# Streaming encoder step: earlier weight splits, an earlier kv norm, keys before queries, and inputs and outputs in pieces of their own

## The chip, the cores and the metric

The kernel runs on one core of one Trainium2 chip. The metric is the device time of one execution in microseconds (us). TensorE (PE) multiplies, VectorE (DVE), ScalarE (ACT) and GpSimd (POOL) do the rest, SyncE (SP) issues the DMAs. Each engine runs its own instructions in the order in which the program emits them, and waits on semaphores for the others.

## What is computed

One layer, on 512 new positions (a prompt) and on 64 new positions that have a past of 128 (a sample): RMSNorm, one input projection, two attention groups side by side, an output projection with a residual, RMSNorm, a gated feed-forward part with a causal convolution, a residual and a last RMSNorm. The second attention group, the latent one, is where most of the change lies:

```python
c_q  = rmsnorm(proj[..., OFF_CQ:OFF_CKV], g_qa)
c_kv = rmsnorm(proj[..., OFF_CKV:OFF_KR], g_kva)
k_r  = rope(proj[..., OFF_KR:IN_COLS], pos)
q_m  = (c_q @ w_qb).reshape(B, T, MLA_HEADS, MLA_NOPE + MLA_ROPE)
q_nope, q_rope = q_m[..., :MLA_NOPE], rope(q_m[..., MLA_NOPE:], pos)
ckv_all = jnp.concatenate([p_ckv, c_kv], axis=1)     # the sample's cache ahead
kv = (ckv_all @ w_kvb).reshape(B, Tk, MLA_HEADS, MLA_NOPE + MLA_V)
k_nope, v_m = kv[..., :MLA_NOPE], kv[..., MLA_NOPE:]
```

## The kernel before

Tokens lie along the free axis: 576 of them (512 and 64), worked on in two groups of 256 and 320 columns (GRP). Every product is made in three passes to keep float32's accuracy: an operand is split into a high part (a cast on ACT) and a low part (the difference, on DVE), and `mm3` (line 136) adds hi x hi, hi x lo and lo x hi in PSUM. So every weight tile of 128x1024 costs two casts on ACT and two subtractions on DVE of 128x512 each (`Weights.split_hi`, line 123, `split_lo`, line 127). A weight has a raw buffer (tag wraw, three of them) and a high and a low one (whi, wlo, four each).

The stages:
1. Lines 195 to 310: the input x (eight tiles of 128 features) and the first key weights are loaded, scaled and split, and the first key pair is multiplied tile by tile (`k_step`, line 263). The squares for the first norm are made beside it.
2. Lines 905 to 1140: 28 attention blocks in slots. A slot combines the block before (softmax scaling), begins a block (scores on PE, maximum on DVE, exponential on ACT), transposes the block before and multiplies values for the one before that. Between these, a planner (`Filler`, line 938) puts the projections that later blocks need, as generators that yield after every few products: V0, K1, Q1, V1, CQ (query latent), CKV (kv latent), KR (rotary key), QU (rotary queries from the latent), U0 to U3 (one head each: queries without rotation and keys, `head_up`, line 716), VM (latent values, `v_up`, line 742), W0 to W3 (output projection).
3. From line 1144 on: the second half of the output projection, the feed-forward part and, in `down(..., last)` from line 1385 on, the last products, the last norm and the stores.

The order on every engine is that of emission as far as stage 2 and again in the last part. In `Filler.step` (line 985) each call counts one step: first the side chains that are due go on by one piece (`beside`, line 972; a chain says with `yield n` in how many steps it wants to go on), then perhaps one half of a weight split is emitted, then the next product. Which weights are split ahead is set by `self.ahead` (those of the next item) and by `SPLIT_EVERY`, every how many steps; what isn't ready when its item begins is split there in one go. `POOL_SPLITS` sends low parts to POOL during CQ and CKV. A weight's load is issued when an earlier weight is ready.

The latent norm is such a side chain (`Latent.normalize`, line 600): squares on ACT, `NORM_STEPS[0]` steps later the column sums on PE (`sum_cols`, line 162: ten matmuls with one column each for one tile of 576), then the root (`rsqrt_cols`, line 171: a memset on POOL, a scaling on DVE, a power on POOL), then a spread over the partitions by PE (`spread`, line 185, tile rbc) and the scaling on DVE, and the split of the result. For kv, `kv_finish` (line 644) first splits the cache part. The rotary key (`rotary_key`, line 651, `shared_key`, line 667) makes two products on DVE and two sums on POOL for each column group (tile kro). Accumulators of tag acc rotate through three PSUM buffers: products, column sums and spreads all use them.

Of the kernel before, what the change touches and what calls it, by code (L numbers as in the profile page):

```python
# [47 lines left out]
Y_GAINS = {4: (0, 2), 5: (2, 3), 6: (3, 4), 7: (4, 5)}  # L48
# [17 lines left out]
def stream_step(ctx: ExitStack, tc: tile.TileContext, i, o):  # L66
# [141 lines left out]
    pieces = [slice(0, 256), slice(256, 512), slice(512, 1024)]  # L208
    w_k = [Weights(i["w_in"][n], 1024, f"wk{n}", pieces) for n in range(2)]
    w_q = [Weights(i["w_in"][2 + n], 1024, f"wq{n}", 2) for n in range(2)]  # L210

    def load_x(c0, c1):
        nc.sync.dma_start(out=xall[:, c0:c1], in_=i["xT"][:, c0:c1])

    def load_tile(k):
        load_x(KD + k * T, KD + (k + 1) * T)
# [12 lines left out]
    w_k[1].load(2)  # L229
    for k in (5, 6, 7):  # L230
        load_tile(k)
# [56 lines left out]
    wsteps = {1: [(0, 1), (1, 1)], 3: [(0, 2)], 4: [(1, 2)]}  # L288
    for k in range(1, KD):
        x_hi(k, full)  # L290
        for n, part in wsteps.get(k, ()):
            w_k[n].split_hi(part)
        if k >= SQUARES_BEHIND:
            square(k - SQUARES_BEHIND)
        x_lo(k, full)
        for n, part in wsteps.get(k, ()):
            w_k[n].split_lo(part)
# [288 lines left out]
    class Latent:  # L586
# [13 lines left out]
        def normalize(self):  # L600
            yield 1
            sqs = []
            for c in self.raws:
                sq = tmp("lsq")
                nc.scalar.activation(out=sq[:, :T], in_=c[:, :T], func=AF.Square)
                sqs.append(sq)
            yield NORM_STEPS[0]
            pc = sum_cols(sqs, T, "acc")
            yield NORM_STEPS[1]
            rc = rsqrt_cols(pc, T, self.n)  # L610
            yield NORM_STEPS[2]
            for c0, cn in GRP:
                pb = spread(rc, c0, cn)
                for m, c in enumerate(self.raws):
                    stt(c[:, c0:c0 + cn], c[:, c0:c0 + cn], vec[:, self.gcol + m:self.gcol + m + 1],
                        pb[:, :cn], ALU.mult, ALU.mult)
                yield NORM_STEPS[3]
# [14 lines left out]
    def q_finish():  # L632
        yield from lat_q.normalize()
# [82 lines left out]
    def head_up(h):  # L716
        if h == 0:
            lw["qns"] = att.tile([P, HEADS, DEC], F32, tag="xs", name="qns")
        ql = lw["qnl", h] = tmp("qnl", (P, SEQ), dt=F32R)
        kl = lw["knl", h] = tmp("knl", (P, SEQ), tag="cs" if h < 2 else "rtab", bufs=2, dt=F32R)  # L720
        for c0, cn in GRP:
# [20 lines left out]
    def v_up(wkv):
        vm = lw["vm"] = att.tile([P, 6, 512], F32, tag="vd", name="vm")
        for t in range(6):
# [6 lines left out]
            nc.scalar.copy(out=vm[:m, t, :], in_=acc[:m])  # L751
# [163 lines left out]
    def w_in(idx, n=2):  # L915
        return [(i["w_in"][idx + m], 1024, f"wi{idx + m}") for m in range(n)]
# [21 lines left out]
    class Filler:  # L938
# [46 lines left out]
        def step(self):  # L985
# [4 lines left out]
            if self.gen is None:  # L990
# [11 lines left out]
                self.finish(*{"QU": ["q"], "U0": ["kv"]}.get(self.name, []))  # L1002
# [391 lines left out]
    def down(s, act, last):  # L1394
# [56 lines left out]
        for f in range(KD):  # L1451
            e0, e1 = Y_GAINS.get(f, (0, 0))

            def before():
                for e in range(e0, e1):
                    scale(1, rn, e, e + 1)
# [6 lines left out]
            if e1 and e1 % 2 == 0:  # L1463
                store(1, e1 - 2, e1)
        scale(1, rn, 5, 6)
        store(1, 4, 6)
        nrm.finish()
        rn0 = nrm.spread()
        scale(1, rn, 6, 8)
        store(1, 6, 8)  # L1470
# [72 lines left out]
def _layout(a):  # L1543
# [3 lines left out]
    d["xT"] = np.ascontiguousarray(np.concatenate(  # L1547
        [a["g_attn"][0].reshape(KD, P).T, x.T.reshape(KD, P, T).transpose(1, 0, 2).reshape(P, KD * T)], 1))
# [9 lines left out]
    d["w_in"] = np.stack([_ktiles(t) for t in tiles])  # L1558
# [18 lines left out]
    for s, n in enumerate(SEGS):  # L1577
# [22 lines left out]
         "conv": (P, NJ, 4), "y": (P, KD, T)}  # L1600
# [25 lines left out]
```

## Time and profile before

| | |
|---|---|
| median of 3 runs | 678.63 us (678.11 to 681.22) |
| profiled execution | 678.01 us |
| its span, first to last instruction | 676.2 us |
| mean granted TensorE clock | 0.992 |
| PE busy | 657.4 us |
| DVE, ACT, POOL busy | 507.3, 314.1, 120.4 us |
| DMA | 63.63 MB, mean 94 GB/s |

How to read it: the span is what the trace covers, and the sum is made against the profiled execution. A PE busy for 97% is bound by its products or by their clock; where it is idle, the list of waits names the engine and line that it waited for. A line can be that of a helper (L84 is every two-operand operation, L87 every one with a scalar, L139 to L141 every three-pass product), so groups go by tile. The granted clock is a share of 2.4 GHz: 1.00 or 0.50 (1.2 GHz), and values between are means over a stretch.

### The profile page before, as it was taken

How to read it: one execution, taken by the hardware profiler on the slowest of the kernel's cores; microseconds unless marked ns; L12 is line 12 of the kernel's file. 1: busy time of each engine (PE TensorE's matmuls, PEld its weight loads, DVE VectorE, ACT ScalarE, POOL GpSimd, SP SyncE). 2: the span in 40 equal slices, each digit the busy share in tenths (PEclk: the TensorE clock that was granted, in tenths of full speed). 3: DMA queues.
4: the chain of work that ended last, by engine and by line, in shares of the span. 5: the costliest groups of instructions: out<-in, count | busy, mean ns of one | idle time of the engine just before them, and what ended most of it. 6: DMA issues, size and time to landing. Idle time of an engine off the chain costs nothing.

```text
span 676.2 us, 12353 instructions
## 1 busy us (share of the span) xinstructions
PE 657.4 (97%) x4830; PEld 632.7 (94%) x4830; DVE 507.3 (75%) x1022; ACT 314.1 (46%) x622; POOL 120.4 (18%) x170
## 2 busy tenths in 40 slices
PE   9999999997899999999999999999999999999995
PEld 8998898996799899999999999999999999999994
DVE  6768866588677757899999849984894788697634
ACT  7324345344634346375565236532640552464263
POOL 0130213034200016232230101210120010011042
PEclk9999999999999999999999999999999999999997
DMA  8564413012514103003133303430431134124103
GB/s 297 176 178 136 133 44 117 12 32 90 200 35 143 45 32 126 1 18 108 63 126 125 126 1 126 125 103 24 126 127 60 48 110 125 36 76 143 32 1 141
DMA packets 26826, 63.63 MB, mean 94 GB/s; under 512 B 3216, under 2 KB 8272, under 8 KB 26768
## 3 DMA queue, kind: packets, MB, share of 16 engines
q1 hardware_dynamic: 26768, 62.84, 28.8%
q8 instruction: 38, 0.62, 0.4%
q14 instruction: 20, 0.16, 0.1%
HBM read 55.27 MB, written 5.21 MB: 89 GB/s over the span
## 4 chain that ended last, share of the span: by engine, by line
PE 85%; DVE 8%; ACT 2%; issue 1%; POOL 1%; DMA 1%; SPq 0%; DVEq 0%; POOLq 0%; ACTq 0%
PE yacc L139 9%; PE yacc L140 9%; PE yacc L141 9%; PE ua L1251 6%; PE ua L1249 6%; PE ua L1250 6%; PE ub L1251 3%; PE ub L1250 3%; PE ub L1249 3%; PE uc L1251 2%; PE uc L1250 2%; PE uc L1249 2%; PE S L490 1%; PE uplain L139 1%; PE tp L467 1%
## 5 line engine op out<-in xcount | busy, mean ns | idle before, releaser
L84 DVE TENSOR_TENSOR x<-x,yacc 128x288 f32<-128x288 f32 (+2 forms) x128 | 56.4, 451 | 49.4 <-PE yacc L141 49.1
L139 PE MATMUL yacc<-act,wd 128*128 128x288 f32 x288 | 85.2, 296 | 0.0
L141 PE MATMUL yacc<-act,wd 128*128 128x288 f32 x288 | 85.1, 296 | 0.0
L140 PE MATMUL yacc<-act,wd 128*128 128x288 f32 x288 | 85.1, 295 | 0.0
L141 PEld LDWEIGHTS yacc<-act,wd 128*128 128x128 f32 x288 | 54.3, 188 | 0.1
L140 PEld LDWEIGHTS yacc<-act,wd 128*128 128x128 f32 x288 | 54.3, 189 | 0.0
L139 PEld LDWEIGHTS yacc<-act,wd 128*128 128x128 f32 x288 | 54.3, 189 | 0.0
L1277 POOL COPY cst<-G 128x2 f32<-128x2 f32 x22 | 19.6, 889 | 164.9 <-DVE G L84 149.0
L458 ACT ACTIVATE p<-S,nmax 128x128 f32<-128x128 f32 (+4 forms) x36 | 18.5, 515 | 42.2 <-DVE nmax L456 41.8
L1338 ACT COPY u<-ua 128x288 f32<-128x288 f32 x20 | 8.0, 399 | 63.9 <-PE ua L1251 63.9
L87 DVE SCALAR_TENSOR_TENSOR conv<-G,vec,conv 128x578 f32<-128x578 f32 x44 | 35.9, 816 | 2.0 <-ACT conv L1282 2.0
L1264 POOL COPY G<-zero 128x2 f32<-128x2 f32 x22 | 14.0, 636 | 130.4 <-DVE conv L87 121.8
L84 POOL TENSOR_TENSOR n<-n,nsq 128x288 f32<-128x288 f32 x13 | 12.3, 950 | 75.3 <-ACT nsq L866 75.1
L1282 ACT ACTIVATE conv<-G,vec 128x578 f32<-128x578 f32 x22 | 19.2, 872 | 8.8 <-DVE G L84 8.7
L458 ACT ACTIVATE p<-Sm,nmax 128x128 f32<-128x128 f32 (+4 forms) x18 | 9.3, 515 | 29.1 <-DVE nmax L456 29.1
L84 POOL TENSOR_TENSOR st<-pr 128x256 f32<-128x256 f32 (+1 forms) x16 | 13.4, 858 | 50.1 <-issue 16.9
L90 ACT CAST act<-conv 128x576 fp32r<-128x576 f32 x22 | 14.9, 675 | 12.7 <-DVE conv L84 12.6
L1286 ACT ACTIVATE silu<-conv 128x578 f32<-128x578 f32 x22 | 15.2, 689 | 11.0 <-DVE conv L87 11.0
L470 DVE COPY pT<-tp 128x128 f32<-128x128 f32 (+3 forms) x36 | 16.7, 463 | 4.3 <-PE tp L467 3.8
L866 ACT ACTIVATE nsq<-x 128x288 f32<-128x288 f32 (+2 forms) x28 | 12.3, 444 | 16.1 <-DVE x L84 16.0
L456 DVE TENSOR_REDUCE nmax<-S 128x1 f32<-128x128 f32 (+4 forms) x36 | 17.0, 476 | 1.1
L467 PE MATMUL tp<-ident,p 128*128 128x128 f32 x84 | 15.5, 277 | 2.3 <-DVE Sm L454 1.0
(1595 smaller groups left out, 2554.8 us busy)
## 6 DMA issues: line engine op xcount, KB each, us to landing
qkT<-st SPq DMA_DIRECT2D x32, 72.0 KB, 2.1
x<-in_xT SPq DMA_DIRECT2D x4, 576.0 KB, 6.4
xraw<-in_xT SPq DMA_DIRECT2D x7, 288.0 KB, 5.3
out_y<-x SPq DMA_DIRECT2D x4, 320.0 KB, 2.3
out_kd<-st SPq DMA_DIRECT2D x4, 288.0 KB, 2.4
out_vp<-vd SPq DMA_DIRECT2D x2, 512.0 KB, 4.7
out_y<-x SPq DMA_DIRECT2D x2, 384.0 KB, 2.7
wq0r<-in_w_in SPq DMA_DIRECT2D x2, 256.0 KB, 5.9
```

The lines of the kernel that those rows point to most:

```text
L84: (eng or nc.vector).tensor_tensor(out=out, in0=a, in1=b, op=op)
L87: nc.vector.scalar_tensor_tensor(out=out, in0=a, scalar=s, in1=b, op0=op0, op1=op1)
L139: nc.tensor.matmul(out, lhsT=wh, rhs=xh, start=first, stop=False)
L140: nc.tensor.matmul(out, lhsT=wh, rhs=xl, start=False, stop=False)
L141: nc.tensor.matmul(out, lhsT=wl, rhs=xh, start=False, stop=last)
L458: nc.scalar.activation(out=p[:, :nk], in_=Sv, func=AF.Exp, bias=nmax[:, 0:1], accum_out=sums)
L467: nc.tensor.transpose(out=pt_ps[:, n * P:n * P + P], in_=a[:, c:c + P], identity=ident)
L1249: nc.tensor.matmul(acc, lhsT=wh, rhs=xh, start=first and n == 0, stop=False, skip_group_check=True)
L1250: nc.tensor.matmul(acc, lhsT=wh, rhs=xl, start=False, stop=False, skip_group_check=True)
L1251: nc.tensor.matmul(acc, lhsT=wl, rhs=xh, start=False, stop=(n == len(ks) - 1), skip_group_check=True)
L1277: nc.gpsimd.tensor_copy(out=cst[:, j, 0:2], in_=G[:, 512:514])
L1282: nc.scalar.activation(out=c[:, :578], in_=G[:, 0:578], func=AF.Identity, scale=cw[0], bias=cb)
```

## The change

1. Weight splits: `POOL_SPLITS` goes, all low parts are on DVE. A table AHEAD names, for CQ to U0, which weights are split during an item, and `SPLIT_EVERY` has other counts.
2. The kv norm has its own, shorter counts, and the split of the cache part is a side chain of its own that begins with the kv products.
3. `head_up` makes the keys of the prompt first, then the queries, then the sample's keys.
4. `v_up` copies its results out of PSUM by ACT and DVE in turn.
5. The input x comes as three tensors, each read at a stretch. The first two key weights come together, two feature tiles at a time from tile 2 on, into buffers of the later softmax. The residual reads x in nine loads, not four.
6. The last scaling writes a tile of its own, in pieces that are contiguous, and each piece is an output tensor. The second group's scalings and stores are done in pairs while the first group's products run.

```diff
-NORM_STEPS = (3, 1, 4, 2)
+NORM_STEPS, KV_STEPS = (3, 1, 4, 2), (2, 1, 3, 1)
-SPLIT_EVERY = {"V1": 3, "U1": 2, "KR": 2, "CKV": 3, "QU": 3, "U0": 2}
-POOL_SPLITS = ("CQ", "CKV")
+SPLIT_EVERY = {"V1": 3, "U1": 2, "CQ": 2, "KR": 2, "QU": 2, "U0": 2}
+AHEAD = {"CQ": ("wi10", "wkr"), "CKV": ("wqr", "wqn"), "KR": ("wkv",), "QU": ("wo0",), "U0": ("wo0",)}
-Y_GAINS = {4: (0, 2), 5: (2, 3), 6: (3, 4), 7: (4, 5)}
+Y_GAINS = {4: (0, 2), 5: (2, 4), 6: (4, 6), 7: (6, 8)}
...
+    def k_load(k, kn=1):
+        nc.sync.dma_start(out=k_cols(k_raw, k, kn), in_=i["w_k1"][k] if kn == 1 else i["w_k2"][k // 2 - 1])
...
-    load_x(0, KD + GRP[1][0])
-    w_k[0].load(0)
-    w_k[1].load(0)
-    load_x(KD + GRP[1][0], KD + T)
+    nc.sync.dma_start(out=xall[:, :KD + GRP[1][0]], in_=i["x_a"])
+    k_load(0)
+    nc.sync.dma_start(out=xraw[:, 0, GRP[1][0]:], in_=i["x_b"])
+    k_load(1)
     load_tile(1)
-    w_k[0].load(1)
-    w_k[1].load(1)
+    k_load(2, 2)
     load_tile(2)
     load_tile(3)
-    w_k[0].load(2)
+    k_load(4, 2)
     load_tile(4)
-    w_k[1].load(2)
-    for k in (5, 6, 7):
-        load_tile(k)
+    load_tile(5)
+    k_load(6, 2)
+    load_tile(6)
+    load_tile(7)
...
-    wsteps = {1: [(0, 1), (1, 1)], 3: [(0, 2)], 4: [(1, 2)]}
+    k_parts = {1: 1, 2: 2, 4: 2, 6: 2}
     for k in range(1, KD):
+        if k in k_parts:
+            k_split_hi(k, k_parts[k])
         x_hi(k, full)
...
-        def normalize(self):
+        def normalize(self, wait):
...
     def kv_latent(ws):
         nc.sync.dma_start(out=kro[:DEC, T:TK], in_=i["c_kr"])
         cc = tmp("cc", (P, P), tag="rd", bufs=2)
         nc.sync.dma_start(out=cc, in_=i["c_ckv"])
+        filler.beside("cc", split_later(ckv[:, 0, T:TK], ckv[:, 1, T:TK], cc))
         yield from lat_kv.project(ws[0])
-        filler.beside("kv", kv_finish(cc))
+        filler.beside("kv", kv_finish())
-    def kv_finish(cc):
-        yield from split_later(ckv[:, 0, T:TK], ckv[:, 1, T:TK], cc)
-        yield from lat_kv.normalize()
+    def kv_finish():
+        yield from lat_kv.normalize(KV_STEPS)
...
+        keys(0, SEQ)
+        yield 3 * SEQ / 2400 + 0.1
         for c0, cn in GRP:
             acc = psum("acc", "qnacc")
...
+        keys(SEQ, PAST + DEC)
+        yield 3 * (PAST + DEC) / 2400 + 0.1
...
-            nc.scalar.copy(out=vm[:m, t, :], in_=acc[:m])
+            if t % 2:
+                nc.vector.tensor_copy(out=vm[:m, t, :], in_=acc[:m])
+            else:
+                nc.scalar.copy(out=vm[:m, t, :], in_=acc[:m])
...
-        for m in range(0, KD, 2):
-            nc.sync.dma_start(out=x1[:, m:m + 2],
-                              in_=i["xT"][:, KD + m * T:KD + (m + 2) * T].rearrange("p (k t) -> p k t", k=2))
+        nc.sync.dma_start(out=x1[:, 0, :GRP[1][0]], in_=i["x_a"][:, KD:])
+        nc.sync.dma_start(out=x1[:, 0, GRP[1][0]:], in_=i["x_b"])
+        for m in range(1, KD):
+            nc.sync.dma_start(out=x1[:, m], in_=i["x"][m - 1])
...
-            if half == w.split_lo and self.name in POOL_SPLITS:
-                half(part, nc.gpsimd)
-            else:
-                half(part)
+            half(part)
...
+                if self.name in AHEAD:
+                    self.ahead = [w for w in self.loaded if w.name in AHEAD[self.name]]
...
+        yo = sb.tile([P, KD * T], F32, tag="M", bufs=2, name="yo")
+        ys = [yo[:, KD * c0:KD * (c0 + cn)].rearrange("p (f t) -> p f t", f=KD) for c0, cn in FG]
...
-            y = x1[:, f:e, c0:c0 + cn]
-            tt(y, y, rn[:, :cn].unsqueeze(1).broadcast_to([P, e - f, cn]), ALU.mult)
+            tt(ys[grp][:, f:e], x1[:, f:e, c0:c0 + cn], rn[:, :cn].unsqueeze(1).broadcast_to([P, e - f, cn]), ALU.mult)
-            nc.sync.dma_start(out=o["y"][:, f:e, c0:c0 + cn], in_=x1[:, f:e, c0:c0 + cn])
+            nc.sync.dma_start(out=o[f"y{grp}_{f}"], in_=ys[grp][:, f:e])
```

## Rows read from the trace of the kernel before

**Rows 1.** The page, part 1: busy us, share of the span, instructions of each engine.

```profile
PE 657.4 (97%) x4830; PEld 632.7 (94%) x4830; DVE 507.3 (75%) x1022; ACT 314.1 (46%) x622; POOL 120.4 (18%) x170
```

**Rows 2.** Stretches: length, busy us of each engine (instructions), PE clock, DMA share, GB/s.

```profile
130.00:140.00 10.00, 10.00 (x72) 8.44 (x72) 5.34 (x16) 3.53 (x8) 2.76 (x4) 1.00 0.03 9
140.00:150.00 10.00, 10.00 (x83) 9.32 (x82) 9.66 (x22) 7.48 (x18) 2.74 (x3) 1.00 0.17 53
150.00:160.00 10.00, 8.13 (x60) 7.64 (x58) 8.70 (x19) 3.53 (x5) 6.27 (x7) 1.00 0.43 152
160.00:170.00 10.00, 8.07 (x45) 6.97 (x44) 7.33 (x19) 4.46 (x15) 3.63 (x4) 0.86 0.09 23
170.00:180.00 10.00, 8.89 (x57) 7.26 (x55) 6.71 (x19) 6.53 (x24) 2.55 (x3) 0.97 0.32 105
```

**Rows 3.** Waits of PE: engine, line, tile, releaser: us in total, times, longest.

```profile
PE qracc L139 <- DVE pr L87: 1.9, 1, 1.9
PE Sm L764 <- ACT knp L738: 1.2, 1, 1.2
...
PE vmacc L748 <- ACT vm L751: 0.6, 1, 0.6
...
PE Sm L765 <- DVE knl L84: 0.4, 1, 0.4
```

**Rows 4.** Stretches of 2 us, as rows 2.

```profile
168.00:170.00 2.00, 2.00 (x8) 1.75 (x8) 1.02 (x4) 0.72 (x4) 0.00 (x0) 0.50 0.43 113
```

**Rows 5.** Timeline of DVE, 146 to 154 us: start, us, instruction [idle before <- releaser].

```profile
146.38 0.68 DVE L84 TENSOR_TENSOR wqrl<-wqrr,wqrh 128x512 fp32r<-128x512 f32 x1
...
147.40 0.43 DVE L84 TENSOR_TENSOR pr<-kracc,sinr 64x256 f32<-64x256 f32 x1
147.86 1.96 DVE L84 TENSOR_TENSOR lat<-lc,lat 128x576 fp32r<-128x576 f32 x2
150.60 0.15 DVE L177 TENSOR_SCALAR ms<-ncol 64x1 f32<-64x1 f32 x1 [0.79 <-POOL ms L176]
...
152.45 1.95 DVE L84 TENSOR_TENSOR wqnl<-wqnr,wqnh 128x512 fp32r<-128x512 f32 x2
```

**Rows 6.** Timeline of PE, KR to the first latent scores.

```profile
145.06 0.36 PE L139 MATMUL kracc<-xh,wkrh 128*128 128x256 f32 x1
...
148.29 1.15 PE L167 MATMUL ncol<-ones,lsq 128*128 128x1 f32 x10
149.37 0.41 PE L139 MATMUL kracc<-xh,wkrh 128*128 128x320 f32 x1
...
151.23 0.28 PE L139 MATMUL qracc<-lat,wqrh 128*128 128x256 f32 x1
...
165.95 0.33 PE L765 MATMUL Sm<-knl,qn 128*128 128x128 f32 x1 [0.40 <-DVE knl L84]
```

**Rows 7.** Timeline of ACT, 145 to 147 us.

```profile
145.39 0.62 ACT L125 CAST wqrh<-wqrr 128x512 fp32r<-128x512 f32 x1
145.90 0.69 ACT L605 ACTIVATE lsq<-lc 128x576 f32<-128x576 f32 x1
```

**Rows 8.** Timeline of POOL, 147 to 153 us.

```profile
147.91 2.50 POOL L84 TENSOR_TENSOR kro<-pr 32x256 f32<-32x256 f32 x2 [7.18 <-DVE pr L84]
150.47 0.10 POOL L176 MEMSET ms<- 128x1 f32 x1
150.97 1.48 POOL L84 TENSOR_TENSOR rc<-ms,mhalf 128x5 f32<-128x5 f32 x1 [0.40 <-DVE ms L179]
```

**Rows 9.** Timeline of ACT at the third x tile.

```profile
8.39 0.78 ACT L252 ACTIVATE xh<-xraw 128x576 fp32r<-128x576 f32 x1 [1.03 <-DMA xraw<-in_xT]
```

**Rows 10.** Stretches of 1 us, as rows 2: head with small and larger pieces, tail.

```profile
5.00:6.00 1.00, 1.00 (x7) 1.00 (x6) 0.55 (x1) 0.20 (x2) 0.00 (x0) 1.00 1.02 281
12.00:13.00 1.00, 1.00 (x10) 1.00 (x9) 0.80 (x2) 1.00 (x3) 0.00 (x0) 1.00 1.03 402
672.00:673.00 1.00, 0.00 (x0) 0.00 (x0) 0.23 (x1) 0.00 (x0) 0.00 (x0) 0.50 1.00 336
```

More of the change, by code (lines that the diff above doesn't have):

```diff
@@ L207, in stream_step, with k_cols, k_split_hi, k_split_lo @@
     xraw = xall[:, KD:].rearrange("p (k t) -> p k t", k=KD)
[L208 to L213, printed above, removed]
-    def load_tile(k):
-        load_x(KD + k * T, KD + (k + 1) * T)
-    load_x(0, KD + GRP[1][0])
-    w_k[0].load(0)
-    w_k[1].load(0)
-    load_x(KD + GRP[1][0], KD + T)
+    k_raw = [att.tile([P, 512], F32, tag="P", bufs=4, name=f"wkr{m}") for m in range(4)]
+    k_hi = [sb.tile([P, 1024], F32R, tag="whi", bufs=4, name=f"wkh{m}") for m in range(2)]
+    k_lo = [sb.tile([P, 1024], F32R, tag="wlo", bufs=4, name=f"wkl{m}") for m in range(2)]
+    w_q = [Weights(i["w_in"][n], 1024, f"wq{n}", 2) for n in range(2)]
+    def k_cols(tiles, k, kn=1):
+        at = k * 256 % tiles[0].shape[1]
+        return tiles[k * 256 // tiles[0].shape[1]][:, at:at + kn * 256]
+    def k_load(k, kn=1):
+        nc.sync.dma_start(out=k_cols(k_raw, k, kn), in_=i["w_k1"][k] if kn == 1 else i["w_k2"][k // 2 - 1])
+    def k_split_hi(k, kn=1):
+        nc.scalar.copy(out=k_cols(k_hi, k, kn), in_=k_cols(k_raw, k, kn))
+    def k_split_lo(k, kn=1):
+        tt(k_cols(k_lo, k, kn), k_cols(k_raw, k, kn), k_cols(k_hi, k, kn).bitcast(F32), ALU.subtract)
+    def load_tile(k):
+        nc.sync.dma_start(out=xraw[:, k], in_=i["x"][k - 1])
+    nc.sync.dma_start(out=xall[:, :KD + GRP[1][0]], in_=i["x_a"])
+    k_load(0)
+    nc.sync.dma_start(out=xraw[:, 0, GRP[1][0]:], in_=i["x_b"])
+    k_load(1)
     load_tile(1)
-    w_k[0].load(1)
-    w_k[1].load(1)
+    k_load(2, 2)
     load_tile(2)
     load_tile(3)
-    w_k[0].load(2)
+    k_load(4, 2)
     load_tile(4)
-    w_k[1].load(2)
-    for k in (5, 6, 7):
-        load_tile(k)
+    load_tile(5)
+    k_load(6, 2)
+    load_tile(6)
+    load_tile(7)
     w_q[0].load(0)
@@ L295, in stream_step @@
         x_lo(k, full)
-        for n, part in wsteps.get(k, ()):
-            w_k[n].split_lo(part)
+        if k in k_parts:
+            k_split_lo(k, k_parts[k])
         if k > ADDS_BEHIND:
@@ L606, in normalize @@
                 sqs.append(sq)
-            yield NORM_STEPS[0]
+            yield wait[0]
             pc = sum_cols(sqs, T, "acc")
-            yield NORM_STEPS[1]
+            yield wait[1]
             rc = rsqrt_cols(pc, T, self.n)
-            yield NORM_STEPS[2]
+            yield wait[2]
             for c0, cn in GRP:
@@ L616, in normalize @@
                         pb[:, :cn], ALU.mult, ALU.mult)
-                yield NORM_STEPS[3]
+                yield wait[3]
     lat_q, lat_kv = Latent(256, V_GQ), Latent(128, V_GKV)
@@ L632, in q_finish @@
     def q_finish():
-        yield from lat_q.normalize()
+        yield from lat_q.normalize(NORM_STEPS)
         for m, c in enumerate(lat_q.raws):
@@ L720, in head_up, with keys @@
         kl = lw["knl", h] = tmp("knl", (P, SEQ), tag="cs" if h < 2 else "rtab", bufs=2, dt=F32R)
+        CK = ([ckv[:, 0]], [ckv[:, 1]])
+        def keys(c0, cn):
+            acc = psum("acc", "knacc")
+            gemm(acc[:, :cn], lw["wkv"], h * P, CK, range(1), slice(c0, c0 + cn))
+            if c0:
+                nc.vector.tensor_copy(out=kns[:, h, :], in_=acc[:, :cn])
+            else:
+                hi = knp[:, h, :]
+                nc.scalar.copy(out=hi, in_=acc[:, :cn])
+                tt(kl, acc[:, :cn], hi.bitcast(F32), ALU.subtract)
+        keys(0, SEQ)
+        yield 3 * SEQ / 2400 + 0.1
         for c0, cn in GRP:
@@ L915, in w_in @@
     def w_in(idx, n=2):
-        return [(i["w_in"][idx + m], 1024, f"wi{idx + m}") for m in range(n)]
+        return [(i["w_in"][idx - 2 + m], 1024, f"wi{idx + m}") for m in range(n)]
     def w_v(half):
@@ L1454, in before @@
             def before():
-                for e in range(e0, e1):
-                    scale(1, rn, e, e + 1)
+                if e1:
+                    scale(1, rn, e0, e1)
             project(0, f, nrm, before=before)
@@ L1462, in down @@
                 rn = last.spread()
[L1463 to L1466, printed above, removed]
+            if e1:
+                store(1, e0, e1)
         nrm.finish()
         rn0 = nrm.spread()
[L1469 to L1470 removed]
         for f, e in zip(Y_CUTS[:-1], Y_CUTS[1:]):
@@ L1557, in _layout @@
     tiles += [w_in[:, 1536:1664], w_in[:, 1664:1792], w_in[:, 1792:1920]]
-    d["w_in"] = np.stack([_ktiles(t) for t in tiles])
+    tiles = [_ktiles(t) for t in tiles]
+    w_k = np.stack(tiles[:2]).reshape(2, P, KD, P).transpose(2, 1, 0, 3).reshape(KD, P, 2 * P)
+    d["w_k1"] = np.ascontiguousarray(w_k[:2])
+    d["w_k2"] = np.ascontiguousarray(w_k[2:].reshape(3, 2, P, 2 * P).transpose(0, 2, 1, 3)).reshape(3, P, 4 * P)
+    d["w_in"] = np.stack(tiles[2:])
     swap = (np.arange(64) + 32) % 64
@@ L1599 @@
 _OUTS = {"kd": (4, P, T), "vp": (P, 4, 512), "vs": (DEC, 512), "ckv": (P, T), "kr": (DEC, T),
-         "conv": (P, NJ, 4), "y": (P, KD, T)}
+         "conv": (P, NJ, 4)}
+_PIECES = [(0, f, e) for f, e in zip(Y_CUTS[:-1], Y_CUTS[1:])] + [(1, f, e) for f, e in Y_GAINS.values()]
+_OUTS.update({f"y{grp}_{f}": (P, e - f, FG[grp][1]) for grp, f, e in _PIECES})
 def kernel(**inputs):
@@ L1612 @@
     g = {k: np.asarray(r.results[0]["out_" + k]) for k in _OUTS}
-    y = g["y"].transpose(2, 1, 0).reshape(T, D)
+    y = np.empty((P, KD, T), np.float32)
+    for grp, f, e in _PIECES:
+        y[:, f:e, FG[grp][0]:sum(FG[grp])] = g[f"y{grp}_{f}"]
+    y = y.transpose(2, 1, 0).reshape(T, D)
     kd = g["kd"].reshape(2, 2, 4, 32, T).transpose(4, 0, 2, 1, 3).reshape(T, 4, 2, 64)
```

39 lines of the change are left out of this document (13 added, 26 removed).

## The prediction

> **What bounds the kernel now.** I read the page's share of busy time first, then the stretches of 10 us, then TensorE's waits, then each engine's timeline around the waits. TensorE (PE) is busy for 97% of the span [rows 1], so a change that leaves its products as they are can only win idle time or clock. In the stretches PE has no idle time from 130 to 150 us; from 150 to 180 it is idle for 1.87, 1.93 and 1.11 us, and its granted clock averages 0.86 and 0.97 in the last two [rows 2]. The list of waits says what ended the idle time [rows 3]: 1.9 us before a product of QU (the queries' up-projection), 1.2 and 0.4 us before the first scores of the latent attention (Sm), 0.6 us in the latent values VM. After the idle time before Sm the clock stands at 0.50, the 1.2 GHz level [rows 4]. The loss to it is 10 x 0.14 + 10 x 0.03 = 1.7 us [rows 2]. So the middle holds 3.5 + 0.6 + 1.7 = 5.8 us. Most of it is VectorE (DVE): 9.66 us busy of 10 in the stretch from 140, but 5.34 in the one before [rows 2].
>
> **Weight splits moved earlier.** The low parts of wqn leave the place where PE waits for DVE (1.95 us for two [rows 5]). By the new tables, counted through the planner, wqr and wqn are split in CKV (eight parts in eight steps), wkv in KR, wo0 in QU. CQ gives DVE five low parts in place of POOL's four and one from KR. Each is 0.68 us on DVE, as wqr's are [rows 5]. CQ and CKV have PE full and DVE half empty [rows 2]: cost 0 in CQ. In CKV a low part waits on DVE for its high part on ACT, and that stands behind a softmax; the scores' reductions queue behind the DVE part. This I price below, with the kv norm.
>
> **The kv norm, three to six steps earlier.** Its column sums move from the seventh product of KR to a place before the fourth, its reciprocal root from the eighth step to the fifth, the spread to the eighth. This adds two waits, in order:
> - Sums: PE gets to that place at 145.06 [rows 6]. ACT can start the squares when the softmax ends, at 145.39, for 0.69 us [rows 7]: 146.1, a wait of 1.0 us. Ends: 0.3 us if the wkr part that leaves DVE here moves the softmax up; 2.8 us if four low parts of CKV, 4 x 0.7, push it back. I take 1.0, what the rows give unmoved.
> - Root: sums 1.1 us (148.29 to 149.37) and one product 0.9 us (two from 149.37 to 151.23) [rows 6] bring PE to 148.1. DVE's two rotation products of the key's first group, 0.4 us each, end at 149.1; POOL adds them in 2.5 us, to 151.6. The root's memset and pow stand behind them on POOL, as now: 150.42 to 152.45, so 2.0 us [rows 5, 8]. The root is there at 153.6. PE has one block of attention values (0.6 us, an estimate), a wait of 0.4 us for the accumulator that the rotation frees, and three products, 2.8 us: 151.9. It waits 1.7 us. Ends: 1.2 (POOL without DVE beside it) and 2.2 us.
>
> Queued behind it: DVE's scaling of the sums waits for POOL's memset (the same 0.79 us wait as now [rows 5]), and from 149.1 to 151.7 it holds back both low parts of the q latent, which now run beside POOL. After it DVE has these (1.96 us [rows 5]), the kv scaling 0.5, a wkv part 0.7 and the rotation of the last key group 1.0: 156.1 with the spread at 153.9 in between. QU's first product needs the accumulator that this rotation frees. So QU starts at 156.1, not at 151.23.
>
> **Keys ahead of the queries in each head.** With latent keys finished in QU's second step, the keys' product comes first in U0 and their evacuations run under the queries' products; both waits at Sm go. From QU's start to Sm's second product it is now 165.95 - 151.23 = 14.7 us [rows 6]. Without the waits, 1.9 + 1.2 + 0.4, and the two spreads that now stand ahead (0.9) this is 10.3; I take 9.7, as some of it is DVE work that goes too. Sm: 156.1 + 9.7 = 165.8, **0.2 us gained**. Ends: QU at 154.0 and 9.3 gives 2.7 gained; QU at 157.9 and 10.3 gives 2.2 lost. So the chain is early, but PE pays in KR what it saves in QU.
>
> **Clock.** The waits are then spread over 146 to 156 in pieces of 1.7 us or less; the 1.9 us in QU now, of that size, didn't lower the clock (1.00 in that stretch [rows 2]). The pair before Sm goes: **1.7 us**. Ends: 1.7 lost, if KR's pieces lower it, and 1.7 gained.
>
> **Values by ACT and DVE in turn.** The wait of 0.6 us for ACT goes; three copies of about 0.7 us come to DVE, ahead of a softmax's scaling: **0.5 us** (0 to 0.6).
>
> **Head.** The x tiles and the first weights come in an order with both halves of a weight tile together and in pieces of 2 KB for 1 KB from the third tile on. ACT waits 1.03 us for tile 2, at 8.39 [rows 9]. With 1 KB pieces the engines moved 281 GB/s at a share of 1.02, with larger ones 402 at 1.03 [rows 10]: 0.26 MB saves 0.28 us, and tile 2 is issued one DMA sooner. But ACT is full from 10 to 20, so I take **0.35 us** (0 to 0.7).
> **Tail.** The outputs go from a tile and into tensors of their own, 2 to 3 KB at a stretch for 1 KB. The last megabyte moves at 336 GB/s at a full share [rows 10]; at 402 it would take 2.5 for 3.0 us: **0.45 us** (0 to 0.5). The scalings of the second group run earlier in DVE's gaps, costing nothing there. The chain to the last spread doesn't change.
> The Trainium skill (DMA: Bandwidth & Descriptors, Specifications) has line rate from 512 B on. By that rule these two would be worth 0.1 in place of 0.8 us and the sum 675.5; the trace does not agree: 281 against 402 GB/s [rows 10].
>
> **At no cost:** nine loads of x for the residual, not four, are five more issues on SP, ahead of wo's later loads there; nobody needs the first tile until W0's sums, and the weights behind them have three buffers. If a load of wo did wait, W0's split of wo1 would be late next. The cache part's split (0.3 us each) fits into CKV; ACT may wait some tenths there for its load, behind a softmax that waits longer.
>
> **Sum.** 0.2 + 1.7 + 0.5 + 0.35 + 0.45 = 3.2 us. The profiled execution took 678.01 us (span 676.2 and 1.8 around it), the median of the runs shown is 678.63. So **674.8 us**. About 0.5% (3.4 us; a measurement of this kernel can hardly tell less) separates faster (below 675.2) and slower (above 682.0).
>
> **Rivals.**
> - *No new wait.* KR absorbs the earlier sums and root; all waits go: 3.5 + 1.7 + 0.6 + 0.4 + 0.5 = 6.7 us, 671.3 us. For it: DVE loses some 4 us of splits between 141 and 154. Against: POOL's 2.5 us ahead of the root is in the rows.
> - *Slower: the root behind the key's rotation.* POOL holds the root, the root's memset holds DVE, DVE's queue holds QU. With the sums late by 2.8 us, QU starts at 157.9 and Sm is 2.2 us late. With the clock loss kept, break-even is a start of QU at 165.95 - 10.0 + 1.3 = 157.3. If the idle time in KR lowers the clock once more, 2.2 + 1.7 - 1.3 = 2.6 us are lost: 680.6 us. Against: the present 1.9 us left the clock alone.
> - *The change doesn't do what it says.* The chain is early, but QU's start waits as long and the transfers at both ends were hidden: only part of the clock is won, 677.3 us.
>
> **How the numbers follow.** Forecast 0.41 (seven in ten of it below 675.2, as its ends pull both ways), no new wait 0.24, the third 0.20, slower 0.15 (half of it beyond 682). Faster 0.53, same 0.40, slower 0.07. The range, 670.5 to 680.5, goes from just under the first rival to the second's price.
>
> **What would show it.** Right: in the waits, QU's and Sm's gone, a new one of 1 to 2 us of the spread (rbc) on POOL's rc in KR, one of the sums (ncol) on ACT's squares; DVE waiting for POOL's memset ahead of the q latent's low parts; clock 1.00 throughout 160 to 180. Wrong: the root's wait absent, a clock of 0.50 anywhere in the middle, or PE waiting for softmax in CQ.

## The result and the profile after

The changed kernel took **683.73 us** (median; 682.33 to 685.17), the kernel before, run beside it, 678.37: 1.008 times the time (95% interval 1.0061 to 1.0098), so 5.4 us slower where 3.2 us less were forecast. Its profiled execution took 683.58 us, with a span of 681.7 for 676.2. First part 1 of its page, the busy time of each engine [rows 1]:

```profile
PE 660.1 (97%) x4830; PEld 634.1 (93%) x4830; DVE 511.0 (75%) x1025; ACT 312.3 (46%) x618; POOL 114.2 (17%) x166
```

and its stretches of 10 us [rows 2]:

```profile
130.00:140.00 10.00, 9.86 (x66) 8.95 (x65) 5.20 (x15) 5.79 (x19) 1.07 (x2) 0.83 0.31 105
140.00:150.00 10.00, 9.07 (x63) 6.75 (x62) 8.48 (x23) 3.19 (x10) 1.48 (x1) 1.00 0.19 66
150.00:160.00 10.00, 7.74 (x56) 7.20 (x57) 5.91 (x13) 2.91 (x7) 3.26 (x5) 1.00 0.00 0
160.00:170.00 10.00, 8.12 (x48) 7.43 (x47) 9.53 (x16) 4.82 (x8) 6.06 (x5) 0.86 0.38 127
170.00:180.00 10.00, 9.39 (x65) 8.34 (x63) 5.75 (x17) 6.10 (x22) 1.60 (x2) 0.97 0.76 260
```

PE is busy for 2.7 us more although it makes the same products: the clock fell to 1.2 GHz not once in the middle but twice, and the new fall, from 130 to 140 us, costs 10 x 0.17 = 1.7 us of it. PE is now idle from 140 us on (0.93 and 2.26 us to 160, in KR), and from 160 to 170, in QU, as long as before (1.88). The waits of PE, which answer to [rows 3]:

```profile
PE qracc L140 <- DVE pr L87: 1.8, 1, 1.8
PE rbc L190 <- POOL ms L910: 1.5, 1, 1.5
PE tp L476 <- DVE p L797: 1.4, 1, 1.4
PE ncol L168 <- ACT lsq L614: 1.1, 1, 1.1
```

The waits at Sm and in VM are gone, both forecast waits of KR are there (the list names the memset that follows the root on POOL; the root itself ends at 157.68), and the one in QU, forecast to go, still takes 1.8 us. The timeline of PE in KR and QU [rows 6]:

```profile
150.79 1.26 PE L168 MATMUL ncol<-ones,lsq 128*128 128x1 f32 x10 [1.12 <-ACT lsq L614]
...
157.73 0.43 PE L190 MATMUL rbc<-ident,rc 128*128 128x128 f32 x2 [1.47 <-POOL ms L910]
...
159.39 0.39 PE L140 MATMUL qracc<-lat,wqrh 128*128 128x256 f32 x1
...
165.90 0.39 PE L140 MATMUL qracc<-lat,wqrh 128*128 128x256 f32 x1 [1.84 <-DVE pr L87]
...
172.78 0.28 PE L782 MATMUL Sm<-knl,qn 128*128 128x128 f32 x1
```

The timeline of POOL there [rows 8]:

```profile
153.93 1.52 POOL L84 TENSOR_TENSOR kro<-pr 32x256 f32<-32x256 f32 x2 [11.01 <-DVE pr L84]
155.51 0.10 POOL L177 MEMSET ms<- 128x1 f32 x1
156.01 1.67 POOL L84 TENSOR_TENSOR rc<-ms,mhalf 128x5 f32<-128x5 f32 x1 [0.40 <-DVE ms L180]
...
160.26 1.81 POOL L84 TENSOR_TENSOR kro<-pr 32x320 f32<-32x320 f32 x2 [2.54 <-DVE pr L84]
162.97 2.19 POOL L84 TENSOR_TENSOR kr<-kro,kr 64x704 fp32r<-64x704 f32 x1 [0.90 <-ACT kr L689]
```

The timeline of DVE [rows 5]:

```profile
155.64 0.15 DVE L178 TENSOR_SCALAR ms<-ncol 64x1 f32<-64x1 f32 x1 [1.79 <-POOL ms L177]
...
155.89 1.43 DVE L84 TENSOR_TENSOR lat<-lc,lat 128x576 fp32r<-128x576 f32 x2
...
159.69 0.49 DVE L84 TENSOR_TENSOR pr<-kracc,sinr 64x320 f32<-64x320 f32 x1
...
160.68 0.42 DVE L87 SCALAR_TENSOR_TENSOR pr<-qracc,cos 128x256 f32<-128x256 f32 x1
...
163.55 1.90 DVE L84 TENSOR_TENSOR q<-pr 128x256 f32<-128x256 f32 x1
165.37 0.48 DVE L87 SCALAR_TENSOR_TENSOR pr<-qracc,cos 128x320 f32<-128x320 f32 x1
```

And that of ACT ahead of the column sums [rows 7]:

```profile
149.67 0.41 ACT L467 ACTIVATE p<-S,nmax 128x192 f32<-128x192 f32 x1
149.97 0.20 ACT L467 ACTIVATION_READ_ACCUMULATOR p<-S,nmax 128x1 f32 x1
150.06 0.68 ACT L614 ACTIVATE lsq<-lc 128x576 f32<-128x576 f32 x1
```

KR is the forecast chain, link by link: the squares behind a softmax on ACT, POOL's rotation sums of the key, behind them the memset, for which DVE waits, and the root, for which PE waits. In QU a link shows that the forecast did not have: DVE's addition q<-pr takes 1.90 us while POOL makes kr. The same operation in DVE's timeline of the kernel before, with POOL at rest:

```profile
155.50 0.42 DVE L84 TENSOR_TENSOR q<-pr 128x256 f32<-128x256 f32 x1
```

Cut at the first products of CQ, KR, QU, at the first scores Sm and at W0's first product (tiles lacc, kracc, qracc, Sm, yacc), the timelines give the lengths in us; in brackets what of it the clock took, the sum over slices of 1 us of one less the granted clock:

| run, profiled execution | CQ, CKV | KR | QU to Sm | Sm to W0 |
|---|---|---|---|---|
| before | 32.64 (0) | 10.05 (0) | 14.00 (0) | 24.14 (1.7) |
| after | 35.77 (1.7) | 14.55 (0) | 13.32 (1.7) | 23.13 (0) |
| kv edit taken back (e1) | 34.37 (0) | 10.76 (0) | 12.24 (0) | 23.14 (0) |
| old splits (e2) | 32.65 (0) | 14.10 (1.7) | 12.90 (0) | 26.04 (3.4) |
| kv edit alone (e12) | 32.64 (0) | 14.03 (1.7) | 14.47 (0) | 24.14 (1.7) |
| root ahead (e6) | 34.38 (0) | 14.46 (1.7) | 13.31 (1.7) | 23.15 (0) |
| key's low part on DVE (e9) | 35.89 (1.7) | 14.54 (1.7) | 11.65 (0) | 22.50 (0) |
| both (e13) | 34.39 (0) | 14.43 (1.7) | 11.62 (0) | 22.52 (0) |
| squares on DVE too, old splits (e16) | 34.21 (1.7) | 11.10 (0) | 12.91 (0) | 24.76 (1.7) |

**The clock as a term.** Each run lists its mean granted clock. 94 runs of the kernel before beside four groups of these experiments fall into groups: 12 at 0.997 took 676.4 us on the mean, 35 at 0.994 took 677.6, 19 at 0.992 took 678.2, 17 at 0.990 took 679.5; the other 11 lie between these or just below them. So 0.001 of clock goes with 0.45 us (the slope of all 94). A fall takes about 1.7 us by the windows, which is 0.0025 of the span, and 0.0025 goes with 1.1 us by the slope (an estimate): part of a fall seems to be made good elsewhere. The six runs of the changed kernel stand at 0.9885 in the median, the 94 at 0.994, so some 2.5 of its 5.4 us (an estimate by the same slope) go with the clock. How often the clock falls differs from run to run of one kernel; a comparison of two single profiles can be off by two falls.

### The profile page after: what moved, and what is told of

It reads as the page before. It is cut to its first block, busy times and chain, and to the rows that moved or that the text cites. A ratio compares the mean times of both kernels' runs of the same rounds, so it can differ in the third digit from the quotient of the medians.

```text
span 681.7 us, 12339 instructions
## 1 busy us (share of the span) xinstructions
PE 660.1 (97%) x4830; PEld 634.1 (93%) x4830; DVE 511.0 (75%) x1025; ACT 312.3 (46%) x618; POOL 114.2 (17%) x166
## 4 chain that ended last, share of the span: by engine, by line
PE 81%; DVE 10%; ACT 4%; issue 2%; POOL 1%; DMA 1%; SPq 0%; DVEq 0%; POOLq 0%; ACTq 0%
PE yacc L140 9%; PE yacc L141 9%; PE yacc L142 9%; PE ua L1268 6%; PE ua L1266 6%; PE ua L1267 6%; PE ub L1268 3%; PE ub L1266 3%; PE ub L1267 3%; PE uc L1268 2%; PE uc L1266 2%; PE uc L1267 2%; PE uplain L140 1%; PE uplain L142 1%; PE uplain L141 1%
## 5 line engine op out<-in xcount | busy, mean ns | idle before, releaser
L476 PEld LDWEIGHTS tp<-ident,p 128*128 128x128 f32 x84 | 10.0, 140 | 8.5 <-issue 2.2
```

The costliest lines, as they stand in the source:

```text
L476: nc.tensor.transpose(out=pt_ps[:, n * P:n * P + P], in_=a[:, c:c + P], identity=ident)
```

## The experiments

Every run was timed beside the kernel before. First, one part taken out of the changed kernel, and two parts of it alone.

**e1: the kv edit taken back**; `normalize` goes by NORM_STEPS again.
```diff
-        filler.beside("cc", split_later(ckv[:, 0, T:TK], ckv[:, 1, T:TK], cc))
-        yield from lat_kv.normalize(KV_STEPS)
+        yield from split_later(ckv[:, 0, T:TK], ckv[:, 1, T:TK], cc)
+        yield from lat_kv.normalize()
```


> The changed kernel with the kv norm's old, longer counts and the cache part split again inside the kv chain; all else as changed. Theory A (the earlier root stands behind the key's rotation on POOL and costs KR 4.5 us): the two waits of KR, 1.1 us for the squares and 1.5 us for the spread, are gone, the first product of QU moves forward by 3 to 4 us, and the time falls from 683.7 to about 680.5; as keys now come first in U0 while the kv latent is late, up to 1 us may come back as a wait before the first keys. Theory B (the moved weight splits load VectorE and cost the time, whatever the kv norm does): 683 to 684, with TensorE waiting for VectorE in QU as before.


678.22 us, ratio 1.0 (0.9986 to 1.0014). The whole loss is gone, 2.3 us below theory A's figure, so outside both. The timeline of PE in QU:
```profile
158.23 0.39 PE L140 MATMUL qracc<-lat,wqrh 128*128 128x256 f32 x1 [0.34 <-DVE pr L87]
...
163.24 0.50 PE L141 MATMUL knacc<-lat,wkvh 128*128 128x512 f32 x1 [1.31 <-DVE lat L84]
...
165.87 0.27 PE L782 MATMUL Sm<-knl,qn 128*128 128x128 f32 x1
```
No wait at the spread, 0.3 us where QU waited, the late latent keys cost 1.3 us, and Sm waits for nothing.

**e2: the old tables of splits**, with POOL_SPLITS. **e3: the old inputs and order of the first part.** **e4: the kernel before with the values by ACT and DVE and the new outputs alone.**


> The changed kernel with the old tables of weight splits (low parts on POOL in the two latent projections, wqn split at the start of QU, nothing of wo0 in QU); all else as changed. Theory A (kv norm): the waits in KR stay, and the low parts of wqn come back at QU's start, so 683 to 685. Theory B (splits): the wait of 1.8 us inside QU goes or moves, the clock holds in the kv projection (1.00 from 130 to 140 us, worth 1.7 us), and the time is 680 to 681.

> The changed kernel with the old loads and the old order of the first part; all else as changed. The trace of the changed kernel has its first product of the query projection 0.47 us later than before. If the new input order is the cause, that product is back at 19.7 us and the time is 683.1 to 683.3; if the first part only shifted by chance, no change, 683.7.

> The kernel before with two parts of the change only: latent values out of PSUM by ScalarE and VectorE in turn, and outputs in pieces of their own. If these are worth what the traces suggest (0.6 us for the wait on ScalarE, 0.67 us between the last product and the end), 677.1 against 678.4; if the wait on ScalarE only turns into a later one, 677.7; if neither is on the path, 678.4.


e2: 682.91 us, ratio 1.0069 (1.005 to 1.0087), theory A's end. Its CQ and CKV take 32.65 us as before, with no fall and no wait, so the new splits do cost PE 1.7 us there (e1, e6 and e13 have 34.37 to 34.39 without a fall); elsewhere e2 lost that again, most of all from Sm to W0 (26.04 us). e3: 683.47, 1.0081 (1.0064 to 1.0099): its query projection begins at 19.72 us, as in the kernel before (19.71), and still the order of the inputs neither gains nor costs anything that shows. e4: 677.66, 0.9998 (0.9983 to 1.0013): a gain of a few tenths at most.

**e12: the kernel before with the kv edit alone**, KV_STEPS 2, 1, 3, 1 and the cache part's split of its own.


> The kernel before with the kv norm's edit alone: counts 2, 1, 3, 1 and the cache part beside the kv products. Theory A (the early norm itself costs: sums waiting for the squares, root behind the key's rotation, VectorE behind in QU): slower by 3 to 5 us, 681 to 683. Theory B (it costs only together with the moved splits or with keys first): within 1 us of the kernel before, 677.5 to 679.


683.32 us, ratio 1.0083 (1.0064 to 1.0103): theory A, a little above its range. The waits of PE:
```profile
PE qracc L139 <- DVE pr L87: 2.5, 2, 1.5
PE Sm L764 <- ACT knp L738: 1.4, 1, 1.4
...
PE ncol L167 <- ACT lsq L605: 0.8, 1, 0.8
...
PE rbc L189 <- POOL ms L892: 0.4, 1, 0.4
```
and, in DVE's timeline, its wait for POOL's memset:
```profile
151.78 0.15 DVE L177 TENSOR_SCALAR ms<-ncol 64x1 f32<-64x1 f32 x1 [1.78 <-POOL ms L176]
```
The edit alone costs all of it, and without keys first it wins nothing at Sm.

**e5: the old counts, but the cache part still on its own**, so that the squares begin as early as in the changed kernel.
```diff
-NORM_STEPS, KV_STEPS = (3, 1, 4, 2), (2, 1, 3, 1)
+NORM_STEPS, KV_STEPS = (3, 1, 4, 2), (3, 1, 4, 2)
```


> The changed kernel with the kv norm's old counts (3, 1, 4, 2), but the cache part still split on its own beside the kv products, so that the norm's squares still begin as early as in the changed kernel. It parts the two halves of that edit. Theory A (the shorter counts alone cost the time: sums and root meet POOL's rotation): as without the whole edit, 678 to 679. Theory B (what costs is that the norm's work begins and lands earlier at all, ahead of the key's rotation and QU on VectorE): 680 to 682.5.


681.05 us, 1.0041 (1.0026 to 1.0056): theory B. About half the cost comes from the counts, half from the cache part's split no longer standing ahead of the norm.

**e14: later than before**, the sums two steps later in the kernel before with e4's parts.


> The kernel before with values in turn and the new outputs (677.7 when run alone), and the kv norm's column sums two steps later than before, so in QU rather than in KR. If the time follows the start of the norm (early 683, two to three steps later 681, as before 678), later still frees VectorE and POOL in KR: the wait of 1.9 us inside QU shrinks to 0.5 to 1 us and the time is 676.5 to 677.5. If the old place is where it stops to matter, the latent keys now come late: TensorE waits 1 to 3 us before the keys' product of U0, 679 to 681.


678.97 us, 1.0019 (1.0006 to 1.0032), against 677.66 for the same kernel without it. Neither guess: the keys' product waits for nothing, but QU does for DVE, 1.3, 1.1 and 0.5 us. By place of the norm, from early to late: 683.3 to 683.7, 681.1, 677.5 to 678.4, 679.0. By these medians the old place is the best.

Next, which link of the early norm costs what. **e6: the root with the sums**, ahead of the key's rotation.
```diff
-            yield wait[1]
+            if wait[1]:
+                yield wait[1]
...
-NORM_STEPS, KV_STEPS = (3, 1, 4, 2), (2, 1, 3, 1)
+NORM_STEPS, KV_STEPS = (3, 1, 4, 2), (2, 0, 4, 1)
```


> The changed kernel with the kv norm's root emitted in the same step as its column sums, ahead of the key's rotation on VectorE and POOL; the spread stays in its step. Theory A (the root waits behind POOL's two rotation sums): the wait of 1.5 us before the spread is gone, VectorE no longer waits 1.8 us for POOL's memset, QU's first product comes 1.5 us or more earlier, and the wait of 1.8 us inside QU shrinks as VectorE is less behind: 680.5 (679.5 to 682). Theory B (QU's wait is set by VectorE's own work): the 1.5 us only move into QU's wait, 683 to 684.


683.03 us, 1.0083 (1.007 to 1.0097). The timeline of POOL:
```profile
152.01 1.49 POOL L84 TENSOR_TENSOR rc<-ms,mhalf 128x5 f32<-128x5 f32 x1 [9.57 <-DVE ms L180]
153.46 0.09 POOL L911 MEMSET ms<- 128x1 f32 x1
153.51 2.41 POOL L84 TENSOR_TENSOR kro<-pr 32x256 f32<-32x256 f32 x2
```
that of PE:
```profile
157.16 0.38 PE L190 MATMUL rbc<-ident,rc 128*128 128x128 f32 x2
...
165.27 0.39 PE L140 MATMUL qracc<-lat,wqrh 128*128 128x256 f32 x1 [1.84 <-DVE pr L87]
```
and the stretch of KR:
```profile
150.00:160.00 10.00, 9.72 (x59) 9.29 (x60) 6.43 (x13) 2.40 (x5) 4.19 (x5) 0.83 0.03 6
```
The wait at the spread is gone, as theory A has it, and the time is theory B's: QU waits the same 1.84 us, and the clock fell in KR, where it had not in the changed kernel. KR takes 14.46 us, the fall in it, for 14.55 without one.

**e7: the key's rotation sums on DVE.** **e8: no split of wo0 in QU.**


> The changed kernel with the two rotation sums of the key (tile kro) on VectorE, not on POOL, for both column groups. Theory A (POOL's rotation holds the root): POOL does the root at once, the spread waits for nothing, 680.5 to 681.5, VectorE having 4 additions of 0.4 to 0.5 us more. Theory B (VectorE's queue sets QU): the 1.7 us more on VectorE are paid in QU, 684 to 685.

> The changed kernel without the splits of wo0 during QU (two casts and two low parts of 0.67 us go from QU to later items). Theory A (the root first, QU's wait follows from it): KR is as before the edit, QU's wait of 1.84 us shrinks by at most 0.7 us: 683. Theory B (VectorE's work inside QU sets the wait there): the wait is gone, and with it the fall of the clock after it: 680 to 681. In both, W0 may pay up to 1 us where wo0 is split later.


e7: 682.25 us, 1.007 (1.0051 to 1.009): between the two; the wait at the spread shrinks to 0.6 us, the 1.8 us in QU stay. e8: 685.29, 1.0101 (1.0081 to 1.0121): outside both. QU's wait shrinks to 1.3 us, within theory A's bound, but after Sm, where wo0 is now split, PE waits 1.8 and 2.0 us for softmaxes on DVE.

**e9: the low part of the rotary key on DVE.**
```diff
-        tt(kr[:DEC, 1, :], kro[:DEC], kr.bitcast(F32)[:DEC, 0, :], ALU.subtract, nc.gpsimd)
+        tt(kr[:DEC, 1, :], kro[:DEC], kr.bitcast(F32)[:DEC, 0, :], ALU.subtract)
```


> The changed kernel with the low part of the rotary key (64x704, tile kr) on VectorE, not on POOL. In the changed kernel VectorE's addition q<-pr of 256 columns takes 1.90 us at 163.55 while POOL makes kr, against 0.42 us alone in the kernel before, and TensorE waits 1.84 us behind it. Theory A (the wait inside QU comes from VectorE being slowed beside POOL): the addition takes 0.4 to 0.5 us, the wait inside QU is 0.5 us or less, and the time falls by 1 to 3 us, to 680.5 to 682.5, the more if the clock no longer falls after it. Theory B (VectorE has too much work there, at any speed): its work grows by 0.8 us, and the time is 683.5 to 684.5.


681.90 us, 1.0065 (1.0044 to 1.0085): theory A. The timeline of DVE in QU:
```profile
163.71 0.41 DVE L84 TENSOR_TENSOR q<-pr 128x256 f32<-128x256 f32 x1
...
166.03 0.87 DVE L84 TENSOR_TENSOR kr<-kro,kr 64x704 fp32r<-64x704 f32 x1
```
the wait of PE that was 1.84 us:
```profile
PE qracc L140 <- DVE pr L87: 0.4, 1, 0.4
```
and the stretch in which the clock no longer falls:
```profile
160.00:170.00 10.00, 9.32 (x62) 8.14 (x60) 9.49 (x18) 5.96 (x11) 3.26 (x4) 1.00 0.44 129
```
DVE has 0.87 us more to do and is done earlier: the addition takes 0.41 us alone and took 1.90 beside POOL. The Trainium skill (SBUF — State Buffer, SBUF: two separate sides) says that DVE and GpSimd share a port pair, which a DVE operation with two inputs in SBUF and a GpSimd operation that reads SBUF hold in turn, each for its whole instruction. The trace agrees: the addition, begun 0.58 us after POOL's 2.19 us of kr, ends 0.29 us after it, while the product pr at 160.68, which reads PSUM, keeps its 0.42 us beside POOL's kro. Beside POOL's root it does not agree: the two low parts lat of 155.89 take 1.43 us during the 1.67 of rc, where the same two took 1.96 beside kro [rows 5, 8].

**e13: e6 and e9 together.** **e15: the same with the old splits and inputs. e16: e15 with the kv squares on DVE.**


> The changed kernel with two repairs at once: the kv norm's root emitted with its column sums, and the low part of the rotary key on VectorE. Alone they gave 683.0 and 681.9 against 683.7. Theory A (the early norm costs by two separate waits on TensorE, at the spread and inside QU): they add up, 680 to 681. Theory B (taking away one wait only moves the loss, into other waits or into the clock): 681.5 to 683.

> The early kv norm with both repairs (root with the sums, low part of the key on VectorE), keys first, values in turn and new outputs, but the splits and inputs of the kernel before. Theory A (the early norm is sound once POOL is out of its way): both waits at the first scores are gone, the one inside QU is under 1 us, 676 to 677.5. Theory B (the early norm costs by its place alone: squares not ready, spreads in KR, VectorE behind): 680 to 682.

> The run before (old splits, both repairs) with the kv squares on VectorE instead of ScalarE, where they stand behind a softmax. Theory A (the wait of 0.8 to 1.1 us for the squares is real loss): that wait is gone and the time 0.8 to 1.1 us under the run before it; where the clock falls less often after it, up to 2 us. Theory B (TensorE waits at the next place instead, for VectorE, which has 0.7 us more): no change within 0.5 us.


e13: 680.94 us, 1.0045 (1.003 to 1.006), in theory A's range. Under the changed kernel's 683.73 the repairs give 0.7 and 1.8 us alone and 2.8 together; against the kernel before beside each, 0.3, 0.9 and 2.2, each within about 1 us. That they add up fits, but e6 alone is no gain clear of noise. e15: 680.54, 1.0035 (1.0016 to 1.0054), theory B's time; inside QU PE waits 1.5 us. e16: 680.53, 1.0032 (1.0016 to 1.0047), theory B. In e16 the column sums wait for nothing and KR is down to 11.10 us, 1.05 over the kernel before, which is what moves there from QU: the spreads, 0.4 + 0.6 us. The norm's own waits are cured, the one inside QU is 1.5 us (1.9 before), and it is still 2.7 us slower than the kernel before. Its mean clock over the runs is lower: median 0.989, and 0.990 in e15, for 0.994 in the 34 runs of the kernel before beside them. By 0.45 us for 0.001, 0.005 goes with 2.3 us, nearly all of e16's 2.7 (an estimate). Two stretches of its profile with a fall, neither in KR:
```profile
130.00:140.00 10.00, 10.00 (x67) 9.09 (x67) 3.76 (x11) 4.65 (x15) 1.07 (x2) 0.83 0.04 10
...
170.00:180.00 10.00, 8.13 (x50) 7.11 (x48) 7.20 (x21) 6.10 (x24) 2.56 (x3) 0.84 0.25 80
```

Last, versions meant to be faster. **e10: the changed kernel without the kv edit and the new inputs, CQ's splits as before. e11: the kernel before with keys first, values in turn and the new outputs.**


> A version meant to be below both: the changed kernel without the new kv norm and without the new input order, and with CQ's splits as before (low parts on POOL, one part each step); wqr and wqn split in CKV, wkv in KR, keys first, values in turn, and the new outputs kept. In the run without the kv edit, TensorE needed 34.37 us from the first product of CQ to the first of KR, with the old splits 32.65. Theory A (the new splits in CQ cost 1.7 us there): 32.7 to 33.2 us for that stretch and 676.0 to 677.0 us in all. Theory B (the splits of CKV are what costs): 34 us for the stretch and 677.5 to 678.5.

> The kernel before with keys first, values in turn and the new outputs, but its own splits, kv norm and inputs. Theory A (keys first takes away the waits of 1.2 and 0.4 us before the first scores even with the kv norm where it was, because the latent keys are ready late but the evacuation is covered): 676.0 to 677.0 against 678.1. Theory B (without the earlier kv norm the wait only moves, from before the scores to before the keys' product, 1.3 us): 677.5 to 678.


e10: 677.31 us, 0.9996 (0.9984 to 1.0008). Its stretch of CQ and CKV is 35.18 us with one fall. A fall made this stretch 1.0 to 1.6 us longer in kernels with the same splits, so it is 33.6 to 34.2 without (an estimate), nearer to theory B; the total is between the two. e11: 678.86, 1.0023 (1.001 to 1.0036), slower than both theories: PE waits 1.1 us for the latent keys and 1.9 us for a later softmax, and the median of its mean clock is 0.990 for 0.994. It bears on e15 and e16, which are e11 with the early norm and its repairs: of their 2.7 us, e11 has 1.4 without any early norm. No version tried is measurably below the kernel before.

## Why the prediction was wrong

The forecast of 674.8 us, from 678.01, is 8.8 us under the profiled 683.58. By stretches, 3.7 us of it lie between QU's start and Sm, 3.1 in CQ and CKV, 1.8 from Sm to W0 and 0.9 ahead of CQ; KR came 0.4 shorter than forecast, and what follows W0 0.5. Step by step:

- **Splits at no cost in CQ: wrong.** CQ and CKV were to stay and took 3.13 us more. 1.7 of it are the splits (34.37 for 32.65 us, neither with a fall); the other 1.4 come with a fall of the clock, which e4's profile has there too, with the old splits. Of the 1.7, PE is idle for 0.6 us, before transposes that wait for a softmax on DVE; the rest is not traced. "DVE half empty" was true and not enough: a part of a split can stand on DVE ahead of a softmax for which PE's transposes wait.
- **The kv norm's two waits: right, the sum in part by luck.** Sums 1.1 us (forecast 1.0), spread 1.5 (1.7), DVE behind the memset 1.8 us. From KR's first product to QU's 14.55 us for 10.05: 4.5 us later, forecast 4.9 (156.1 for 151.23). But QU's first product did not wait for the rotation of the last key group, as the forecast had it: it began at 159.39, and that rotation's last reading of kracc ran on DVE from 159.69 to 160.18. The sums began 1.0 us further into KR than the forecast put them, which made up for most of what that saved.
- **From QU's start to Sm 9.7 us: the step that failed.** It took 13.39 (172.78 - 159.39), 3.7 us more: 1.84 are the wait inside QU and 1.7 the fall of the clock behind it. "Some of it is DVE work that goes too" took QU's wait of 1.9 us off. DVE's later work did not go: the kv latent's low part, wo0's parts and the additions for q now run in QU beside POOL's kr, at more than four times their length for one; the wait moved from QU's third product to its sixth and stayed at 1.84 us. e9 shows it: with the addition at 0.41 us wait and fall are gone, and waits of 0.4, 0.3 and 0.6 us for DVE are left, so QU to Sm took 11.65 for 13.32 us. The forecast named this price for POOL, "without DVE beside it", and did not ask it of DVE. Sm's waits did go, so keys first worked as described. The sign of DVE's price stood in the forecast's own rows: two low parts of wqn took 1.95 us [rows 5], where it counted 0.68 for each, and POOL's timeline of the kernel before has the key's sums beside them:

```profile
152.50 2.62 POOL L84 TENSOR_TENSOR kro<-pr 32x320 f32<-32x320 f32 x2
```

- **Clock, 1.7 us regained: wrong in the mechanism.** "The 1.9 us in QU now, of that size, didn't lower the clock" was taken as a rule from one profile. After the same wait it fell here, at 167 us, and in e6 and e13 it fell in KR with the wait at the spread gone. Falls vary between runs of one kernel, so one profile bears no term of 1.7 us; by the 94 runs a fall goes with 1.1 us.
- **Values in turn, 0.5 us:** VM's wait is gone, but from the second product of Sm to W0 it took 23.06 us for 23.42, with a whole fall of 1.7 less: other waits for DVE, 1.4 us before a transpose, took its place. e4 puts this and the outputs together at a few tenths.
- **Head, 0.35 us: not there.** The query projection began 0.47 us later, not earlier (in e1, with the same inputs, 0.17 earlier), and e3 finds no difference in the whole time.
- **Tail, 0.45 us: right.** The last scalings go out at up to 393 GB/s, where 336 stood before [rows 10] and 344 at most; a stretch of 1 us:

```profile
678.00:679.00 1.00, 0.00 (x0) 0.00 (x0) 0.14 (x1) 0.00 (x0) 0.00 (x0) 0.50 1.00 393
```
From the start of the last spread to the end of the span it is 681.7 - 675.3 = 6.4 us for 676.2 - 669.3 = 6.9; the tile rbc in the changed kernel (durations, first and last start):
```profile
L190 PE MATMUL rbc<-ident,rc x21: 237/272/323, 144.7 to 675.3; 128*128 128x128 f32 x16, 64*128 64x64 f32 x3, 32*128 32x32 f32 x2
```
and in the kernel before:
```profile
L189 PE MATMUL rbc<-ident,rc x21: 237/271/473, 141.0 to 669.3; 128*128 128x128 f32 x16, 64*128 64x64 f32 x3, 32*128 32x32 f32 x2
```

Of the rivals, "the root behind the key's rotation" (680.6 us, 0.15) was nearest, with its break-even point in KR; it had the right links and, like the forecast, no second price in QU. Taken alone, the root gave nothing clear of noise (e6), and the squares nothing at all (e16 against e15). Its counter-argument, "the present 1.9 us left the clock alone", is what fell.

What is shown: the loss is the kv edit's (e1, e12); its waits are the squares, the root and DVE slowed beside POOL, and with repairs for all three (e16) about 2.7 us over the kernel before remain, at a lower mean clock. Of these, 1.4 are there without the early norm (e11), so what is left of the norm's own cost, some 1.3 us, is not clear of noise. The lower clock is not the norm's alone either: e11 has it, e1 and e10 do not (0.994 and 0.995). What stays open: why the clock falls more often in these kernels. In the profiles with the early norm it fell in KR in e2, e3, e6, e8, e9, e12, e13 and e15, not in after, e5, e7 and e16; in the six without it (before, e1, e4, e10, e11, e14) never in KR. That is a count, not a cause.

## What to carry to other kernels

A chain of small steps that is brought forward lands somewhere: price what its engines do at the new place as they run there, beside the neighbour that slows them, and not as they ran alone. Before a clock loss is booked as a gain, look at the mean granted clock of all runs: a term that comes and goes between runs of one kernel is no saving, and a wait taken away can be followed by a fall in its stretch (e6). When an edit has several parts, measure each alone first; here five parts summed to nothing that shows (e1), and the sixth alone gave the whole result (e12).

## What was not expected of the hardware

DVE's addition of 128x256 took 1.90 us beside a POOL operation of 2.19 and 0.41 alone. The granted clock fell to 0.50 with hardly any idle time before it (0.14 us from 130 to 140 us): PE had just made 20 column sums of one column each, in its timeline of the changed kernel

```profile
134.36 2.16 PE L168 MATMUL ncol<-ones,lsq 128*128 128x1 f32 x20
```

when the clock stood at 0.50, in a stretch of 1 us:

```profile
137.00:138.00 1.00, 1.00 (x6) 1.00 (x5) 0.28 (x1) 0.00 (x0) 0.00 (x0) 0.50 0.13 29
```

The same sums in the kernel before, at 132.63 us, left it at 1.00 in the profile shown. In ten of the eighteen profiles the clock falls soon after these sums, in eight it does not; what decides it stays open.
